# The opening of a hybrid attention / DeltaNet layer on one core: another order of modulation vectors, transposes and first projections

## The chip, the core and the metric

The kernel runs on one core of a Trainium2 chip. A core has TensorE (PE in the profile; its weight loads are PEld), VectorE (DVE), ScalarE (ACT), GpSimd (POOL), and SyncE (SP), which here only starts transfers. Each engine works through its own instructions in a fixed order and waits at an instruction until the inputs of that instruction are there. The metric is the device time of one execution in microseconds (us).

## The reference, cut to what matters

The program is one layer over 512 latent tokens `x` and 256 context tokens `ctx`, 1024 channels wide, in float32. The change is in the very first part of it: the modulation vectors, the modulated normalised inputs, and the beginning of the big input projection.

```python
mod_lat = jax.nn.silu(c) @ w_mod + b_mod              # 1024 -> 6 x 1024
mod_ctx = jax.nn.silu(c_ctx) @ w_mod + b_mod
sh1, sc1, g1, sh2, sc2, g2 = jnp.split(mod_lat, 6, axis=-1)
csh1, csc1, ... = jnp.split(mod_ctx, 6, axis=-1)

hx = rms_norm(x)   * (1.0 + sc1)  + sh1               # (512, 1024)
hc = rms_norm(ctx) * (1.0 + csc1) + csh1              # (256, 1024)
... = split_cols(hx @ w_in)                           # attention q/k/v, DeltaNet q/k/v, decays, gates
... = split_cols(hc @ w_in[:, :CTX_COLS])
```

Behind that stand grouped-query attention, a bidirectional chunked DeltaNet, the merge of both, an output projection, a gated MLP with a short convolution, and a final RMSNorm. Nothing of that part is changed.

## The kernel before, in words

Every product of the projections is made of three matmuls, because a float32 operand is taken as a high part and a low part: `hi` is a copy in the format that TensorE reads (ScalarE, line 127), `lo` is the difference (line 115, VectorE, or GpSimd where an engine is named). The helper `split` (line 129) does both, and `mm3` issues the three matmuls `w_hi x_hi`, `w_hi x_lo`, `w_lo x_hi`. A weight tile is 128 x 1024; its parts are called `whi` and `wlo`, what was loaded is `wraw`.

The opening (lines 440 to 605) goes through these steps, and each has a letter in the string `ORD`, which sets the order in which TensorE's work of the opening is issued. TensorE's instructions are pinned to that order; on the other engines a scheduler orders the instructions by priority when the program is built, and on the SP queue the loads are pinned to the order of `LORD`.

- Loads, by SP, in the order `x0 x1 x2 w0 w1 h0 h1 w2 .. w7`: the context and the two halves of `x` (tiles `xs`, 1 MB each), the first third of `w_mod` in eight tiles `wm` of 1 MB, and two weight tiles `h0`, `h1` of the projection. Then the rotary tables (`tabs`), `wrow`, and, in a place that the scheduler chooses, the masks (`cst`, line 474). Eight transfers can be on the way; the ninth waits for the first.
- Each `xs` tile holds two rows of tokens per partition. ScalarE squares and sums the one row, VectorE the other (lines 487, 488), VectorE and GpSimd make the reciprocal root `rs` (the power is on GpSimd, line 115), and VectorE scales both rows (line 493).
- `xN` (N from 0 to 11): TensorE transposes four 128 x 128 blocks of an `xs` tile into a PSUM tile `pt`; ScalarE or VectorE copies them to a stash (`hxL`, `hcL`). There are two `pt` buffers. `x0` to `x3` are the context, `x4` to `x7` the first and `x8` to `x11` the second half of the tokens.
- `aN`, `bN`: the two halves of the vector product number N (0 to 3) of `silu(c)`, `silu(c_ctx)` with 512 columns of `w_mod` (`pm`); after `bN` ScalarE copies the result into `mrow`. Product N needs the tiles `wm` 2N and 2N+1. There is one `pm` buffer.
- `mN`: makes columns (one value per partition) of the row `mrow`: four matmuls against a 0/1 matrix `sel` into `xb`, which also add up the four partial sums, and two additions of the bias (`mod`, `modc`).
- `yN`: the modulation of the channel pair N (channels 256N to 256N+255): `hf` for the latent tokens on VectorE, for the context on ScalarE, then the split of four tiles (`hxH`, `hcH` on ScalarE, `hxL`, `hcL` on VectorE).
- `pK` (K from 0 to 7): the matmuls of both projection tiles (heads) with channel block K: for each head three on the context (`pc`, 256 columns) and three on the latent tokens (`mb`, 512 columns). `qK` and `rK` are the halves of `pK` for head 0 and head 1; the string of before uses neither.
- `dN`: 4N matmuls on zeros, whose result nobody uses.

So the products of a channel block need the modulation of that block, that needs its columns, these the vector product, and that two tiles of `w_mod`. After the last product `p7`, convolution taps are read from the PSUM tiles by ScalarE and VectorE, and TensorE goes on with the attention's K, V and Q blocks (`pq`).

Of the kernel before, what the change touches and what calls it, by code (L numbers as in the profile page):

```python
# [16 lines left out]
KT = 8  # L17
# [17 lines left out]
POOLW = 0  # L35
ND, D0U = 4, 6
KV = 10
ORD = 'd4 x0 x1 x2 x3 x4 x5 x6 x7 a0 x8 x9 x10 x11 b0 d1 m0 y0 a1 p0 b1 p1 m1 y1 a2 b2 p2 m2 y2 p3 a3 b3 p4 m3 y3 p5 p6 p7'
RK = 1.0
HB = 2  # L40
WS = [1.0, 1.0, 1.0]
# [34 lines left out]
def hybrid_layer_body(tc, x, ctxt, xT, consts, cols, rows, w_mod1, w_mod2, w_av, w_aq, w_cm, w_pa, w_pd, w_out,  # L76
# [64 lines left out]
    with es:  # L141
# [299 lines left out]
        with m1_es:  # L441
# [11 lines left out]
            for op in LORD.split():  # L453
                i = int(op[1])
                with sooner():
                    if op[0] == "w":
                        wms.append(m1.tile([P, 4, 512], F32, name="wm", tag="in", bufs=WB))
                        ordered_load(wms[i], w_mod1[i // 2, i % 2])
                    elif op[0] == "h":
                        h, part = order[i]  # L460
                        raw = ws.tile([P, 1024], F32, name="wraw", tag="wraw", bufs=2)
                        ordered_load(raw, w_cm[8 * part + h])
                    else:
                        xs.append(m1.tile([P, 2, D], F32, name="xs", tag="in", bufs=WB))
                        ordered_load(xs[i], x[:, 2 * i - 2:2 * i, :] if i else ctxt)
                if op[0] == "h":
                    with first():
                        hi, lo = (m1.tile([P, 1024], F32R, name=n, tag=n, bufs=NS) for n in ("whi", "wlo"))
                        split(hi, lo, raw)
                        hw.append((hi, lo))  # L470
            with sooner():
                ordered_load(tabs.rearrange("p a b -> p (a b)"), consts[:, C_COS:C_END])
                ordered_load(wrow, rows[0:512].partition_broadcast(P))
            SP.dma_start(cst[:, C_MS:C_TRI], consts[:, C_MS:C_TRI])
            cs = m1.tile([P, 16], F32, name="cs")
            act(cs, col[:, S_C:S_C + 16], AF.Tanh, scale=0.5)
            stt(cs, cs, 1.0, col[:, S_C:S_C + 16], ALU.add, ALU.mult)
            cs32 = m1.tile([P, KT, 32], F32, name="cs32")
            G.memset(cs32, 0.0)
            ts(cs32[:, :, 0:2], cs.rearrange("p (k two) -> p k two", two=2), 0.5, ALU.mult)  # L480
            sel = m1.tile([P, 2], F32, name="sel")
            V.tensor_reduce(out=sel, in_=ident.rearrange("p (b c) -> p c b", c=32)[:, 0:2, :], axis=AX.X, op=ALU.add)
            ss = m1.tile([P, 6], F32, name="ss")
            rs = m1.tile([P, 6], F32, name="rs")
            for i in range(3):
# [4 lines left out]
                sl = slice(2 * i, 2 * i + 2)  # L490
                rsqrt(rs[:, sl], ss[:, sl], 1.0 / D, EPS)
                for t in range(2):
                    ts(xs[i][:, t, :], xs[i][:, t, :], rs[:, 2 * i + t:2 * i + t + 1], ALU.mult)
            m2 = lambda t, o: t[:, o:o + 16].rearrange("p (s k) -> p s k", s=2)
            wsl = lambda k: slice(k * P, k * P + P)

# [9 lines left out]
                    act(mrows[nb], ps)  # L506

            def mod_cols(nb, mrow):
                pst = xbank()[:, 0, 0:8].rearrange("p (a b) -> p a b", b=2)
                for i in range(4):  # L510
                    mm(pst[:, i, :], mrow[:, i * P:(i + 1) * P], sel)
                ks = slice(2 * nb, 2 * nb + 2)
                p4 = pst.rearrange("p (s k) r -> p s k r", s=2)
                for j, md in enumerate((mod, modc)):
                    tt(m2(md, 0)[:, :, ks], p4[:, :, :, j], m2(col, S_BMOD)[:, :, ks], ALU.add)

# [35 lines left out]
            def early_proj(k, heads=slice(0, NS)):  # L552
                if not hps:
                    for _ in range(NS):
                        hps.append((mbank(), mps.tile([P, NCX], F32, name="pc", tag="pc", bufs=NS)))
                for (ps, pc), (hi, lo) in list(zip(hps, hw))[heads]:
                    mm3(pc, hi[:, wsl(k)], lo[:, wsl(k)], hcH[:, k, :], hcL[:, k, :], k, KT)
                    mm3(ps, hi[:, wsl(k)], lo[:, wsl(k)], hxH[:, k, :], hxL[:, k, :], k, KT)

            pinned[0] = True  # L560
            mrows, mpm = {}, {}
# [1113 lines left out]
```

## Time and profile before

| | |
|---|---|
| median of 3 runs | 1242.44 us (1237.12 to 1246.0) |
| the profiled execution | 1239.93 us, of which the span from the first to the last instruction is 1238.2 us |
| granted TensorE clock, mean | 0.986 |
| busy time | PE 1183.2 us (96%), DVE 818.8 (66%), ACT 601.7 (49%), POOL 248.3 (20%) |
| the opening ends (last matmul of `p7` out, `pq` starts) | near 56 us of the span |

A row of the timeline gives start, duration, engine, line, operation, output and input tiles, shapes and a count, and in square brackets the idle time of the engine just before it with what ended it. A row of a stage gives for each engine its busy time and the number of instructions, then the granted TensorE clock (1.00 is full), the share of the time in which the DMA engines were busy, and the rate in GB/s. Matmuls overlap: the duration of one is longer than its distance from the next. Line numbers in rows are those of the kernel before.

### The profile page before, as it was taken

What the parts mean: (1) busy time and instruction counts of PE and PEld (TensorE: products, weight loads), DVE (VectorE), ACT (ScalarE), POOL (GpSimd) and SP (SyncE); (2) the same over time, 40 slices, a digit from 0 to 9 for tenths busy, and PEclk for the clock granted to TensorE, in tenths of its full rate; (3) what the DMA queues carried; (4) which work ended last, traced back from release to release, by engine and by line L of the source; (5) the groups of instructions that cost most, each with busy time, mean ns of one, the idle gap of its engine ahead of it and who ended that gap; (6) DMA issues with size and microseconds to landing.
All of it is one profiled execution on the core that took longest, in us unless ns stands there. A gap on an engine that the chain in (4) does not pass through costs nothing.

```text
span 1238.2 us, 20489 instructions
## 1 busy us (share of the span) xinstructions
PE 1183.2 (96%) x7753; PEld 1015.6 (82%) x7753; DVE 818.8 (66%) x1611; ACT 601.7 (49%) x1386; POOL 248.3 (20%) x334
## 2 busy tenths in 40 slices
PE   7999899999899898999999989999999999999996
PEld 5799888989787787788887678789888888888886
DVE  5648678888698657766657677866776765553333
ACT  4524477877565845744535432333544444432321
POOL 0111110100314695595574000000000000000000
PEclk8999999999999998999999999999999999999998
DMA  9413313332536426335336776862333422333331
GB/s 385 143 60 117 99 56 97 113 100 89 191 130 213 132 90 205 116 122 194 129 97 202 243 251 204 304 223 103 119 122 133 136 93 95 102 92 97 94 94 68
DMA packets 67554, 174.97 MB, mean 141 GB/s; under 512 B 7456, under 2 KB 18176, under 8 KB 66048
## 3 DMA queue, kind: packets, MB, share of 16 engines
q1 hardware_dynamic: 67456, 173.67, 41.8%
q8 instruction: 61, 1.00, 0.3%
q14 instruction: 37, 0.30, 0.1%
HBM read 146.85 MB, written 26.79 MB: 140 GB/s over the span
## 4 chain that ended last, share of the span: by engine, by line
PE 53%; DMA 4%; DVE 4%; ACT 2%; issue 1%; POOL 1%; SPq 0%; POOLq 0%; DVEq 0%; ACTq 0%
PE mc L84 33%; PE mb L84 13%; PE pb L84 5%; DMA gt<-atd 1%; DVE wlo L115 1%; DMA M<-gamdr 1%; PE pk L84 1%; ACT whi L127 0%; DMA wl<-in_w_mod_dram 0%; PE pqk L84 0%; DMA sz<-gdr 0%; POOL NN L115 0%; DMA cw<-in_rows_dram 0%; DMA Gb<-gamdr 0%; DMA NN<-gamdr 0%
## 5 line engine op out<-in xcount | busy, mean ns | idle before, releaser
L115 DVE TENSOR_TENSOR wlo<-wraw,whi 128x1024 fp32r<-128x1024 f32 (+1 forms) x153 | 188.7, 1235 | 159.9 <-ACT whi L127 159.5
L127 ACT ACTIVATE whi<-wraw 128x1024 fp32r<-128x1024 f32 (+1 forms) x153 | 159.5, 1044 | 213.8 <-PE mc L84 114.0
L84 PE MATMUL mc<-h,whi 128*128 128x512 f32 (+1 forms) x752 | 219.6, 376 | 0.3 <-ACT whi L127 0.3
L84 PE MATMUL mb<-hxH,whi 128*128 128x512 f32 x384 | 162.5, 423 | 1.6 <-DVE t L124 1.6
L84 PEld LDWEIGHTS mc<-h,whi 128*128 128x128 f32 x752 | 138.0, 188 | 26.1 <-ACT whi L127 0.5
L84 PE MATMUL mb<-hxL,whi 128*128 128x512 f32 x384 | 152.2, 396 | 0.2 <-DVE hxL L115 0.2
L84 PE MATMUL mb<-hxH,wlo 128*128 128x512 f32 x384 | 152.2, 396 | 0.0
L84 PE MATMUL mc<-h,wlo 128*128 128x512 f32 (+1 forms) x376 | 141.3, 376 | 0.5 <-DVE wlo L115 0.5
L84 PE MATMUL mc<-a,whi 128*128 128x512 f32 (+1 forms) x396 | 111.1, 366 | 0.6 <-DVE x L124 0.6
L115 POOL TENSOR_TENSOR rc<-rc,mhalf 128x2 f32<-128x2 f32 x4 | 3.0, 740 | 456.8 <-DVE rc L121 456.8
L84 PEld LDWEIGHTS mb<-hxH,wlo 128*128 128x128 f32 x384 | 73.0, 190 | 16.8
L84 PEld LDWEIGHTS mb<-hxH,whi 128*128 128x128 f32 x384 | 73.4, 191 | 11.9 <-issue 2.0
L84 PEld LDWEIGHTS mc<-a,whi 128*128 128x128 f32 x396 | 71.5, 189 | 12.9 <-DVE x L124 0.8
L84 PEld LDWEIGHTS mc<-h,wlo 128*128 128x128 f32 x376 | 70.8, 188 | 13.6 <-DVE wlo L115 1.0
L84 PEld LDWEIGHTS mb<-hxL,whi 128*128 128x128 f32 x384 | 73.5, 191 | 9.7 <-DVE hxL L115 0.5
L84 PE MATMUL mc<-a,wlo 128*128 128x512 f32 (+1 forms) x198 | 72.3, 365 | 0.0
L124 DVE SCALAR_TENSOR_TENSOR u<-mc,col,u 128x511 f32<-128x511 f32 x88 | 65.3, 746 | 1.4
L115 POOL TENSOR_TENSOR prod<-X,R 128x31 f32<-128x31 f32 (+15 forms) x93 | 55.5, 597 | 19.1 <-DVE X L115 12.3
L115 POOL TENSOR_TENSOR R<-R,prod 128x31 f32<-128x31 f32 (+15 forms) x93 | 56.5, 607 | 6.8
L84 PE MATMUL pq<-whi,hxH 128*128 128x256 f32 (+1 forms) x192 | 55.5, 289 | 0.0
L84 PE MATMUL pq<-wlo,hxH 128*128 128x256 f32 (+1 forms) x192 | 54.3, 283 | 0.1
L84 PE MATMUL pq<-whi,hxL 128*128 128x256 f32 (+1 forms) x192 | 54.2, 282 | 0.0
(323 smaller groups left out, 2692.1 us busy)
## 6 DMA issues: line engine op xcount, KB each, us to landing
wraw<-in_w_cm_dram SPq DMA_DIRECT2D x48, 512.0 KB, 3.6
wraw<-in_w_up_dram SPq DMA_DIRECT2D x44, 512.0 KB, 3.3
wl<-in_w_mod_dram SPq DMA_DIRECT2D x24, 512.0 KB, 4.9
wm<-in_w_mod_dram SPq DMA_DIRECT2D x8, 1024.0 KB, 16.6
wraw<-in_w_down_dram SPq DMA_DIRECT2D x16, 512.0 KB, 3.5
wraw<-in_w_aq_dram SPq DMA_DIRECT2D x10, 512.0 KB, 3.8
M<-gamdr SPq DMA_DIRECT2D x64, 64.0 KB, 4.5
wraw<-in_w_pa_dram SPq DMA_DIRECT2D x8, 512.0 KB, 4.4
```

The source lines that it names most:

```text
L84: i = nc.tensor.matmul(*a, **k)
L115: put((eng or V).tensor_tensor(out=out, in0=a, in1=b, op=op))
L124: V.scalar_tensor_tensor(out=out, in0=a, scalar=s, in1=b, op0=op0, op1=op1)
L127: put(A.activation(out, a, f, **kw))
```

## The change

Five edits, all in the opening.

- `ORD` is another string. There are 28 matmuls on zeros ahead of `x0` instead of 16, and the four of `d1` stand behind `x3` instead of behind `b0`. `b0` stands behind `x8`, ahead of `x9`; `m0` and `y0` stand behind `x9`, ahead of `x10` and `x11`. From then on both halves of a vector product stand ahead of the products they used to follow: `p0 a1 b1`, and the column form `m1` comes between the two heads of the product `p1` (`q1 m1 y1 r1`); so with `m2` and `m3`.
- The column form: instead of four matmuls with `sel`, four transposes of 128 x 128 blocks of `mrow` into one PSUM tile, then one VectorE sum over the four partial rows into `m4`, and the two bias additions read `m4`. `sel` and the reduction that made it are gone.
- The scaling of the second row of each `xs` tile is on GpSimd; the first stays on VectorE.
- The low part of the weight tile `h0` is made on GpSimd; that of `h1` stays on VectorE.
- The masks are loaded behind `wrow`, pinned in the SP order. Within `pK`, `qK` and `rK` the latent products come first, those on the context second.

```diff
-ORD = 'd4 x0 x1 x2 x3 x4 x5 x6 x7 a0 x8 x9 x10 x11 b0 d1 m0 y0 a1 p0 b1 p1 m1 y1 a2 b2 p2 m2 y2 p3 a3 b3 p4 m3 y3 p5 p6 p7'
+ORD = 'd7 x0 x1 x2 x3 d1 x4 x5 x6 x7 a0 x8 b0 x9 m0 y0 x10 x11 p0 a1 b1 q1 m1 y1 r1 a2 p2 b2 q3 m2 y2 r3 a3 p4 b3 q5 m3 y3 r5 p6 p7'
@@ loads of the weight tiles h0, h1
-                        split(hi, lo, raw)
+                        act(hi, raw)
+                        tt(lo, raw, hi, ALU.subtract, V if hw else G)
                         hw.append((hi, lo))
@@ masks
-            SP.dma_start(cst[:, C_MS:C_TRI], consts[:, C_MS:C_TRI])
+                ordered_load(cst[:, C_MS:C_TRI], consts[:, C_MS:C_TRI])
@@ sel
-            sel = m1.tile([P, 2], F32, name="sel")
-            V.tensor_reduce(out=sel, in_=ident.rearrange("p (b c) -> p c b", c=32)[:, 0:2, :], axis=AX.X, op=ALU.add)
@@ scaling of xs
-                    ts(xs[i][:, t, :], xs[i][:, t, :], rs[:, 2 * i + t:2 * i + t + 1], ALU.mult)
+                    ts(xs[i][:, t, :], xs[i][:, t, :], rs[:, 2 * i + t:2 * i + t + 1], ALU.mult, eng=G if t else V)
@@ mod_cols
-                pst = xbank()[:, 0, 0:8].rearrange("p (a b) -> p a b", b=2)
+                pst = xbank()
                 for i in range(4):
-                    mm(pst[:, i, :], mrow[:, i * P:(i + 1) * P], sel)
+                    transpose(pst[:, i, :], mrow[:, i * P:(i + 1) * P])
+                m4 = m1.tile([P, 4, 2], F32, name="m4", tag="m4", bufs=2)
+                V.tensor_reduce(out=m4, in_=pst.rearrange("p i (b c) -> p i c b", c=32)[:, :, 0:2, :], axis=AX.X, op=ALU.add)
                 ks = slice(2 * nb, 2 * nb + 2)
-                p4 = pst.rearrange("p (s k) r -> p s k r", s=2)
+                p4 = m4.rearrange("p (s k) r -> p s k r", s=2)
@@ early_proj
-                for (ps, pc), (hi, lo) in list(zip(hps, hw))[heads]:
+                some = list(zip(hps, hw))[heads]
+                for (ps, pc), (hi, lo) in some:
+                    mm3(ps, hi[:, wsl(k)], lo[:, wsl(k)], hxH[:, k, :], hxL[:, k, :], k, KT)
+                for (ps, pc), (hi, lo) in some:
                     mm3(pc, hi[:, wsl(k)], lo[:, wsl(k)], hcH[:, k, :], hcL[:, k, :], k, KT)
-                    mm3(ps, hi[:, wsl(k)], lo[:, wsl(k)], hxH[:, k, :], hxL[:, k, :], k, KT)
```

Three places of the built order, before and after. First VectorE at the beginning, around the first column form; `hxL<-pt` are copies of transposes, `wlo` is the low part of a weight tile, `mod` and `modc` are the columns. Before:

```order
L119 TENSOR_SCALAR xs<-xs,rs 128x1024 x2
L531 COPY hxL<-pt 128x2x256 x2
L115 TENSOR_TENSOR wlo<-wraw,whi 128x1024 x2
L115 TENSOR_TENSOR mod<-xb,col 128x2x2
L115 TENSOR_TENSOR modc<-xb,col 128x2x2
L121 TENSOR_SCALAR hf<-hxL,mod 128x512 x2
```

Now:

```order
L119 TENSOR_SCALAR xs<-xs,rs 128x1024
L532 COPY hxL<-pt 128x2x256 x2
L115 TENSOR_TENSOR wlo<-wraw,whi 128x1024
L512 TENSOR_REDUCE m_402<-xb 128x8
L115 TENSOR_TENSOR mod<-m_402,col 128x2x2
L115 TENSOR_TENSOR modc<-m_402,col 128x2x2
L532 COPY hxL<-pt 128x2x256
L121 TENSOR_SCALAR hf<-hxL,mod 128x512 x2
```

One of the two weight differences and one scaling have gone from this stretch (to GpSimd), the new sum `m4` (shown as `m_402`) stands behind the other weight difference, and one copy of transposes now stands between the columns and the modulation `hf`.

Second TensorE behind the second column form `m1`. Before, both halves of the next vector product and then the products of the next pair follow it:

```order
L84 MATMUL xb<-sel,mrow 128x2 x4
L84 MATMUL pm<-wm,cs_259 32x512 x8
L84 MATMUL pc<-hcH,whi 128x256
L84 MATMUL pc<-hcL,whi 128x256
L84 MATMUL pc<-hcH,wlo 128x256
```

Now one head's products of the pair before, half a vector product, and then the next pair:

```order
L88 MATMUL xb<-cst,mrow 128x128 x4
L84 MATMUL mb<-hxH,whi 128x512
L84 MATMUL mb<-hxL,whi 128x512
L84 MATMUL mb<-hxH,wlo 128x512
L84 MATMUL pc<-hcH,whi 128x256
L84 MATMUL pc<-hcL,whi 128x256
L84 MATMUL pc<-hcH,wlo 128x256
L84 MATMUL pm<-wm,cs_259 32x512 x4
L84 MATMUL mb<-hxH,whi 128x512
```

What stands between the column form and the first product that needs it is another set of instructions.

Third ScalarE in the third and fourth modulation; `whi<-wraw 128x1024` here are the high parts of two weight tiles (`w_aq`) of the K block that comes after the opening. Before, they stand behind the last vector row `mrow`:

```order
L127 ACTIVATE mrow<-pm 128x512
L127 ACTIVATE hf<-hcL,modc 128x256 x2
L127 ACTIVATE hxH<-hf 128x512
L127 ACTIVATE hcH<-hf 128x256
L127 ACTIVATE hxH<-hf 128x512
L127 ACTIVATE hcH<-hf 128x256
L127 ACTIVATE mrow<-pm 128x512
L127 ACTIVATE whi<-wraw 128x1024 x2
```

Now they stand one modulation earlier, the first ahead of it and the second inside it:

```order
L127 ACTIVATE mrow<-pm 128x512
L127 ACTIVATE whi<-wraw 128x1024
L127 ACTIVATE hf<-hcL,modc 128x256 x2
L127 ACTIVATE hxH<-hf 128x512 x2
L127 ACTIVATE whi<-wraw 128x1024
L127 ACTIVATE hcH<-hf 128x256 x2
L127 ACTIVATE whi<-wraw 128x864
L127 ACTIVATE mrow<-pm 128x512
```

VectorE's differences `wlo` of the same tiles have moved with them. Behind `p7` TensorE's order is the same instruction by instruction in both programs; on VectorE and ScalarE a few neighbours are exchanged there.

## The prediction

> **What bounds the kernel now.** I read the page first, then the stages, TensorE's waits, and the timeline. The page's first line:
>
> ```profile
> span 1238.2 us, 20489 instructions
> ```
>
> The profiled execution took 1239.93 us, 1.7 us more than this span. The opening is its first 56 us. The stages (columns: length, busy time of PE, PEld, DVE, ACT, POOL, granted clock, DMA share, GB/s) and, in shorter ones, the clock:
>
> ```profile
> 0.00:9.80 9.80, 5.33 (x16) 3.96 (x17) 3.54 (x12) 3.24 (x5) 1.36 (x10) 1.00 0.80 305
> 9.80:27.04 17.24, 14.85 (x85) 9.21 (x85) 12.45 (x22) 10.41 (x20) 1.40 (x2) 0.80 1.02 422
> 27.04:56.05 29.01, 27.21 (x160) 19.17 (x161) 15.10 (x33) 14.56 (x29) 0.81 (x1) 0.94 0.55 202
> 56.05:140.00 83.95, 83.90 (x699) 83.65 (x698) 57.70 (x206) 35.07 (x132) 13.34 (x13) 1.00 0.26 82
> ...
> 14.70:18.10 3.40, 3.40 (x18) 2.37 (x20) 2.25 (x6) 0.99 (x3) 0.70 (x1) 0.50 1.01 414
> ...
> 28.30:31.80 3.50, 3.50 (x13) 2.18 (x16) 0.38 (x2) 0.00 (x0) 0.00 (x0) 0.51 1.01 417
> ```
>
> To 27.04 us, where the first product starts, transfers run at full rate and TensorE waits for normalised inputs and columns. Behind 56.05 it is busy 83.90 of 83.95 us: nothing there hides or adds to a shift, so a microsecond of the opening is a microsecond of the kernel. From 27.04 to 56.05:
>
> ```profile
> PE pc L84 <- ACT hcH L127: 1.8, 2, 1.3
> PE pc L84 <- DVE hcL L115: 1.1, 3, 0.4
> PE mb L84 <- DVE hxL L115: 0.2, 1, 0.2
> ...
> 33.63 0.28 PE L84 MATMUL pc<-hcH,whi 128*128 128x256 f32 x1
> 34.68 0.95 PE L84 MATMUL xb<-sel,mrow 128*128 128x2 f32 x8
> 35.56 1.92 PE L84 MATMUL pm<-wm,cs 128*32 128x512 f32 x16
> ...
> 1.49 5.33 PE L84 MATMUL pt<-hxH 128*128 128x512 f32 x16 [1.49 <-DVE hxH L563]
> 17.87 1.16 PE L84 MATMUL pm<-wm,cs 128*32 128x512 f32 x8
> 18.96 1.13 PE L88 MATMUL pt<-cst,xs 128*128 128x128 f32 x8
> 21.45 1.06 PE L84 MATMUL pm<-wm,cs 128*32 128x512 f32 x8
> ```
>
> 1.3 us of the first wait lie ahead of 27.04, so 1.8 us of waits are inside. One head of one block takes 34.68 - 33.63 = 1.05 us, a half vector product (1.92 - 0.15 tail)/2 = 0.88, a column form 0.95, four transposes 0.46 and a tail of 0.2. The 29.0 us are 16 x 1.05 = 16.8, plus 6 x 0.88 = 5.3, plus 3 x 0.95 = 2.85, plus 1.7 lost to the clock of 0.51 in 3.5 us, and 2.35 of idle time and gaps. TensorE's own work sets this stage, with its waits well covered.
>
> **Up to the first product.** Prices on ScalarE, VectorE and GpSimd, and the loads that are waited for:
>
> ```profile
> 11.05 1.09 ACT L127 ACTIVATE hcL<-pt 128x512 f32<-128x512 f32 x2 [0.69 <-PE pt L88]
> 13.34 1.05 ACT L127 ACTIVATE hxH<-xs 128x1024 fp32r<-128x1024 f32 x1
> 23.00 0.59 ACT L127 ACTIVATE mrow<-pm 128x512 f32<-128x512 f32 x1
> 25.06 1.09 ACT L127 ACTIVATE hf<-hcL,modc 128x256 f32<-128x256 f32 x2 [1.47 <-DVE modc L115]
> 26.06 0.62 ACT L127 ACTIVATE hxH<-hf 128x512 fp32r<-128x512 f32 x1
> 46.37 2.00 ACT L127 ACTIVATE whi<-wraw 128x1024 fp32r<-128x1024 f32 x2
> ...
> 3.75 0.17 DVE L482 TENSOR_REDUCE sel<-cst 128x2 f32<-128x8 f32 x1 [2.31 <-DMA cst<-in_consts_dram]
> 8.99 1.42 DVE L119 TENSOR_SCALAR xs<-xs,rs 128x1024 f32<-128x1024 f32 x2 [0.82 <-POOL rs L115]
> 21.73 1.22 DVE L115 TENSOR_TENSOR wlo<-wraw,whi 128x1024 fp32r<-128x1024 f32 x1
> 24.74 0.16 DVE L115 TENSOR_TENSOR mod<-xb,col 128x4 f32<-128x4 f32 x1 [0.37 <-PE xb L84]
> 24.94 1.00 DVE L121 TENSOR_SCALAR hf<-hxL,mod 128x512 f32<-128x512 f32 x2
> 26.71 0.69 DVE L115 TENSOR_TENSOR hxL<-hf,hxH 128x512 fp32r<-128x512 f32 x1 [0.77 <-ACT hxH L127]
> ...
> xs<-in_x_dram SPq DMA_DIRECT2D x1, 1024.0 KB, 9.0
> 2.13 0.91 SPq L448 DMA_DIRECT2D xs<-in_x_dram  x2
> ```
>
> The twelve further matmuls on zeros cost nothing: 16 take 5.33 us from 1.49 (12 more at that rate end at 10.8, at the later spacing near 9.4), and x0 is held anyway: on ScalarE the square of the third `xs` tile now stands ahead of the copies of transposes. That tile lands at 2.6 + 9.0 = 11.6, the square ends at 12.7, and the first `pt` buffer is free (copies of 0.5 each) only from 13.3. x2 and x3 follow, then d1; x4 starts at 15.5, and four groups at half clock (to 18.1 as in the row of before; about 0.85 each, a little under twice 0.46) bring a0 to 18.9 instead of 17.87. x8 and b0 follow without x9 to x11: b0 starts at 20.3 instead of 21.45. ScalarE first makes both `whi` (1.0 each, 19.6 to 21.5), then `mrow`, at 21.5 against 23.00; its transposes end at 22.8, where the columns of before were read at 24.74. That gains 1.9 us.
>
> GpSimd's new work is not in this trace in its form. Its nearest rows, and one place where both engines use SBUF:
>
> ```profile
> L990 POOL MEMSET R<- 128x1024 f32 x4 | 3.8, 955 | 0.0
> L1033 POOL COPY TTm<-o_tr 32x384 f32<-32x384 f32 x16 | 9.1, 569 | 1.2 <-PE pb L84 0.5
> L115 POOL TENSOR_TENSOR kA<-tabs,wrow 128x512 f32<-128x512 f32 x1 | 1.3, 1291 | 38.6 <-PE mb L84 38.6
> ...
> 511.37 2.13 DVE L115 TENSOR_TENSOR wlo<-wraw,whi 128x1024 fp32r<-128x1024 f32 x1
> 512.37 2.85 POOL L115 TENSOR_TENSOR NN<-NN,cst 128x768 f32<-128x768 f32 x1
> 516.25 1.85 POOL L115 TENSOR_TENSOR NN<-NN,Gb 128x768 f32<-128x768 f32 x1
> ```
>
> A scaling of 128x1024 lies between a memset of the size (0.96) and a two-input operation, 1.29 per 512 columns or 2.6; I take 1.4, the copy's 0.57 for 384 columns carried on, since it too reads one tensor. The difference `wlo` has two inputs: 1.85/768 x 1024 = 2.45. The last three rows show exclusion: the VectorE difference that takes 1.22 alone took 2.13 beside GpSimd's sums, and GpSimd's next 2.85 instead of 1.85 behind it.
>
> If the scalings exclude each other too, a pair takes up to 0.75 + 1.4; but the copy of x0 waits for 12.7 and x4 for 15.5, which covers it. Exclusion decides at the weight differences: GpSimd's runs from 20.7 to 23.1; VectorE's, whose `whi` is there at 21.6, goes from 23.1 to 24.3, and the sum stands behind it, as VectorE's order shows. The sum has no row; it lies between the 0.17 of the old reduction and the 0.69 of a 512-column operation, and with 8 results out of 32 numbers I take 0.22. Columns at 24.7; then ScalarE's two `hf` (0.55 each), a copy (0.5) and an `hcH` (0.35) stand ahead of `hxH` (0.62): first product at 27.3, 0.3 later than before. Without exclusion the sum is at 22.8 and the first product at 25.9: 1.1 earlier. I take the exclusion.
>
> **From the first product on.** The columns cost 0.46 instead of 0.95, three times: -1.45. The clock first, since it can undo that:
>
> ```profile
> 24.90:28.30 3.40, 1.69 (x12) 0.70 (x5) 2.63 (x8) 2.75 (x6) 0.00 (x0) 1.00 1.02 414
> ```
>
> Before, 1.69 us of work in 3.4 ahead of 28.3 were followed by 3.5 us at half clock. Now TensorE has done x11 by 23.6 and stands still until 27.3, so about 1.1 us of work fall into the same stretch: I take one slow stretch, worth 1.75 us, as before: +0.05.
>
> The idle time grows. From the start of a column form to the first product that needs it pass: transposes 0.65, sum and columns 0.45, two context `hf` on ScalarE 1.05 and `hxH` 0.62, with signals 2.9 us. Before, the work of TensorE that stood there was 0.95 + 1.76 = 2.7 us for m1, 0.95 + 2.1 + 1.76 = 4.8 for m2, 0.95 + 2.1 = 3.05 for m3. Now it is 0.46 + 1.05 + 0.88 = 2.4 for m1 and m2, and 1.5 for m3, behind which no vector product is left. So TensorE stands 0.5, 0.5 and 1.4 us, and each time 0.55 more after one matmul, until the low part `hxL` (0.69) is made. In y2 the K weights come in between, as ScalarE's order shows:
>
> ```profile
> 24.18 2.81 SPq L214 DMA_DIRECT2D wraw<-in_w_aq_dram  x2
> ...
> wraw<-in_w_aq_dram SPq DMA_DIRECT2D x1, 512.0 KB, 15.9
> ```
>
> The first lands at 24.18 + 15.9 = 40.1 (the bytes ahead of it are the same, since the masks only move behind `wrow`), ScalarE copies it at 41.6, behind the third `mrow`, so nobody waits for the load; but the two VectorE differences of 1.22 stand ahead of `hxL` and of the context's low part, so p4 waits 0.3 more for the one and 0.85 for the other. Idle: 0.55 (p0), 1.05 (p2), 2.2 (p4), 1.9 (p6), together 5.6 before rounding. I walked both orders through engine by engine, with these durations and 0.05 us for a signal; for the order of before this ends the opening at 56.0, where the trace has 56.05. For the new order: 27.3 + 16.8 + 5.3 + 1.4 + 1.75 + 5.6 = 58.15. The sum: start +0.3, columns -1.45, clock +0.05, idle and gaps 5.6 - 2.35 = +3.25: **+2.1 us**, 0.2% of the kernel.
>
> At nothing: the masks, which nothing in the opening reads; the order latent before context in `p`, the same matmuls; the SP queue, whose loads stand behind a backlog of 15 us anyway (w5 to w7 come 0.6 us earlier, and b3 runs near 48, 12 us behind them).
>
> [...]
>
> **The rivals.** *Faster:* no exclusion between the engines. First product at 25.9, 1.1 earlier, and with 2.1 us of work ahead of 28.3 the clock may stay full. But then ScalarE reaches the copy of the K weights before 40.1 and waits: the end is 56.0, and 54.9 if the tile lands a microsecond sooner, 54.0 with a full clock from 14.7 on: 0 to -2 us. For it: one-input work on GpSimd isn't seen beside VectorE here; against: two-input work is, and the weight difference is that. *Slower, by GpSimd's chain:* each power for `rs` now stands behind the scaling of the tile before on GpSimd, so three scalings in a row lead to x8 and to the first columns. From about 3 us for a scaling this chain is the later one, and each further microsecond costs three; 1% (12.4 us) is reached near 6. The longest row that compares, 1.29 for half the size with two inputs, makes 2.6, and the end 59.0: +2.9. [...] *Not what it says:* if y0 needed x9 to x11, an earlier b0 would gain nothing; but y0 reads what x0, x4 and x8 left, so the edit holds: chance 0.
>
> **The numbers.** Forecast, +2.1 (from +1 to +3): 0.5; faster, 0 to -2: 0.33; slow clock 0.12; GpSimd's chain beyond +3: 0.05. Against the profiled 1239.93 that is 1242.0, against the median, 2.5 above it, 1244.5; I give 1243, between the two. The three runs spread from 1237.12 to 1246.0, so the range is 1237.12 - 1 to 1246.0 + 3: 1236 to 1249. A measurement tells about 1%, 12.4 us, from no change. Even with the first product at 25.9 and no idle time behind it the opening would end at 25.9 + 23.5 = 49.4, 6.7 us earlier, so faster by 1% can only come from outside the opening: 0.02. Slower by 1% needs GpSimd at 6 us: 0.03. Same: 0.95.
>
> **What would show it.** In the profile after: the third square ahead of the first copy on ScalarE; a GpSimd scaling of 1.0 to 2.6 us; VectorE's first weight difference near 2.4 us, or starting when GpSimd's ends; first product at 27 to 28 us; a granted clock of 0.50 for one window behind it; TensorE idle for 5 to 6 us between there and `pq`, most of it at p4 and p6; `pq` at 57 to 59 us. A first product at 26 us with `pq` at 56 or earlier would show the faster rival, one behind 29 the chain on GpSimd. The prediction is wrong if `pq` starts below 54 or above 61, or if the time differs by more than the opening's end does.

## The result, and the profile after

The changed kernel takes 1248.05 us (median of 11 runs, 1245.34 to 1249.7), the kernel before 1239.71 us (11 runs): a ratio of 1.0065, 95% interval 1.0051 to 1.0078, or 6.3 to 9.7 us more. The forecast was 1243, in a range that holds the result; the +2.1 us of its working are a quarter of the 8.1 measured.

The profiled execution of after took 1246.63 us. First the page's first line, then the stages (length, busy time of PE, PEld, DVE, ACT, POOL, granted clock, DMA share, GB/s), cut at the first product and at the first `pq` as before:

```profile
span 1244.9 us, 20486 instructions
...
9.80:29.83 20.03, 13.11 (x76) 8.90 (x74) 12.11 (x20) 10.98 (x20) 13.78 (x6) 0.83 1.02 422
29.83:61.26 31.43, 28.23 (x157) 18.54 (x158) 15.39 (x34) 14.47 (x28) 0.18 (x1) 0.95 0.43 152
61.26:145.21 83.95, 82.74 (x690) 82.36 (x689) 58.52 (x206) 34.49 (x127) 14.00 (x13) 1.00 0.25 82
```

The first product starts at 29.83 instead of 27.04 (+2.8; forecast 27.3), `pq` at 61.26 instead of 56.28 (the first `pq` matmul; +5.0; the forecast's 58.15 was worked against 56.05). GpSimd, 1.40 us busy in the second stage before, is now busy 13.78 of 20.03 us. Behind the opening TensorE, which was busy 83.90 of 83.95 us, is idle for 1.2 us. The waits of TensorE (us in total, times, longest) in and just behind the products:

```profile
PE mb L84 <- ACT hxH L127: 4.9, 4, 3.2
...
PE pq L84 <- DVE rk L121: 1.2, 1, 1.2
...
PE mb L84 <- DVE hxL L115: 1.0, 3, 0.5
```

3.2 of the first lie ahead of 29.83. The second is new, and stands in no step of the prediction. The start, in the order of time (start, length, engine, line; POOL is GpSimd; from here on the line numbers of a row are those of the kernel that it comes from):

```profile
8.31 0.70 POOL L115 TENSOR_TENSOR rs<-rs,mhalf 128x2 f32<-128x2 f32 x1 [7.13 <-DVE rs L121]
9.04 0.75 DVE L119 TENSOR_SCALAR xs<-xs,rs 128x1024 f32<-128x1024 f32 x1 [0.81 <-POOL rs L115]
9.11 4.46 POOL L119 TENSOR_SCALAR xs<-xs,rs 128x1024 f32<-128x1024 f32 x1
...
11.05 0.80 DVE L121 TENSOR_SCALAR rs<-ss 128x2 f32<-128x2 f32 x1
...
13.54 0.72 POOL L115 TENSOR_TENSOR rs<-rs,mhalf 128x2 f32<-128x2 f32 x1
13.62 3.56 PE L88 MATMUL pt<-cst,xs 128*128 128x128 f32 x15 [3.23 <-POOL xs L119]
...
14.37 3.41 POOL L119 TENSOR_SCALAR xs<-xs,rs 128x1024 f32<-128x1024 f32 x1
...
17.74 0.72 POOL L115 TENSOR_TENSOR rs<-rs,mhalf 128x2 f32<-128x2 f32 x1
18.56 2.85 POOL L119 TENSOR_SCALAR xs<-xs,rs 128x1024 f32<-128x1024 f32 x1
...
23.45 2.37 POOL L115 TENSOR_TENSOR wlo<-wraw,whi 128x1024 fp32r<-128x1024 f32 x1 [2.04 <-ACT whi L127]
...
24.35 2.55 DVE L115 TENSOR_TENSOR wlo<-wraw,whi 128x1024 fp32r<-128x1024 f32 x1 [0.25 <-ACT whi L127]
24.44 0.60 ACT L127 ACTIVATE mrow<-pm 128x512 f32<-128x512 f32 x1
...
26.83 0.18 DVE L512 TENSOR_REDUCE m<-xb 128x8 f32<-128x32 f32 x1
```

GpSimd's scalings take 4.46, 3.41 and 2.85 us, and the powers `rs` stand between them at 8.31, 13.54 and 17.74: one chain on one engine. The transposes of the context wait 3.23 us for its first link. At the end VectorE's weight difference takes 2.55 us beside GpSimd's, and the sum stands behind it, as the prediction had it.

One profiled execution below, that of the first experiment, was disturbed (its clock was 0.84 on average), so only its times are used; the other thirteen traces are used whole.

### The profile page after: what moved, and what is told of

Same layout as the page of the kernel before. It is cut to its first block, busy times and chain, and to the rows that moved or that the text cites. A ratio compares the mean times of both kernels' runs of the same rounds, so it can differ in the third digit from the quotient of the medians.

```text
span 1244.9 us, 20486 instructions
## 1 busy us (share of the span) xinstructions
PE 1188.7 (95%) x7749; PEld 1020.5 (82%) x7749; DVE 819.1 (66%) x1610; ACT 601.2 (48%) x1386; POOL 262.5 (21%) x338
## 4 chain that ended last, share of the span: by engine, by line
PE 53%; DVE 4%; DMA 3%; issue 1%; POOL 1%; ACT 1%; SPq 0%; POOLq 0%; DVEq 0%; ACTq 0%
PE mc L84 33%; PE mb L84 13%; PE pb L84 6%; DMA wl<-in_w_mod_dram 1%; DVE wlo L115 1%; PE pk L84 1%; PE pqk L84 0%; DMA szd<-co 0%; DMA gt<-atd 0%; DMA M<-gamdr 0%; POOL NN L115 0%; DVE o_tr L1016 0%; DMA sz<-gdr 0%; ACT whi L127 0%; DMA cw<-in_rows_dram 0%
## 5 line engine op out<-in xcount | busy, mean ns | idle before, releaser
L115 DVE TENSOR_TENSOR wlo<-wraw,whi 128x1024 fp32r<-128x1024 f32 (+1 forms) x152 | 188.8, 1243 | 157.0 <-ACT whi L127 154.5
L84 PE MATMUL mb<-hxH,whi 128*128 128x512 f32 x384 | 165.3, 430 | 6.5 <-ACT hxH L127 4.9
L115 POOL TENSOR_TENSOR prod<-X,R 128x31 f32<-128x31 f32 (+15 forms) x93 | 53.3, 573 | 19.8 <-DVE X L115 12.9
L124 DVE SCALAR_TENSOR_TENSOR t<-mb,col,t 128x511 f32<-128x511 f32 (+1 forms) x76 | 48.9, 644 | 9.7 <-ACT t L127 9.4
```

Of the source, the lines that this page charges most:

```text
L84: i = nc.tensor.matmul(*a, **k)
L115: put((eng or V).tensor_tensor(out=out, in0=a, in1=b, op=op))
L124: V.scalar_tensor_tensor(out=out, in0=a, scalar=s, in1=b, op0=op0, op1=op1)
```

## The experiments

Each is after, or before, with one thing changed, or two or three where its name says so. The table has, for each, the ratio to before with its 95% interval (before ran again beside the experiments, after did not), and from its trace the start of the first product and of `pq`, and what the time between them leaves when its work is taken off: 16 x 1.05 for the products, 0.88 for each half vector product (5.3 for six in the new order of steps, 4.4 for five in the old one), three column forms (2.85, or 1.4 with transposes), and half of the time that the clock stood at 0.5 in between (an estimate: in before the next latent matmul of a row starts 0.42 us behind the last one there, 0.23 to 0.24 at full clock). The sixth half, `a1`, stands ahead of the first product in the old order, here in before, where that product starts at 27.04:

```profile
24.63 1.06 PE L84 MATMUL pm<-wm,cs 128*32 128x512 f32 x8
```

The prediction's sum for before takes off six. The rest is idle time and gaps. It is more than the idle time of the profile, which grows from 1.8 us (29.01 - 27.21) to 3.2 (31.43 - 28.23): a latent matmul ahead of a wait counts as busy for 0.49 us, though in a row the next one starts 0.23 behind it.

| kernel | ratio (interval) | first product | `pq` | clock at 0.5 between, us | rest, us |
|---|---|---|---|---|---|
| before | 1 | 27.04 | 56.28 | 3.4 | 3.5 |
| after | 1.0065 (1.0051 to 1.0078) | 29.83 | 61.26 | 3.4 | 6.2 |
| after, scalings on VectorE | 1.0028 (1.0012 to 1.0044) | - | - | - | - |
| after, weight differences on VectorE | 1.0042 (1.0025 to 1.0058) | 28.35 | 59.88 | 3.4 | 6.3 |
| after, both on VectorE | 1.0038 (1.0024 to 1.0053) | 27.91 | 59.93 | 3.4 | 6.8 |
| after, both on VectorE, context first | 1.0051 (1.0032 to 1.0070) | 25.08 | 61.40 | 6.8 | 9.4 |
| after, context first | 1.0050 (1.0030 to 1.0071) | 28.98 | 64.67 | 10.2 | 7.1 |
| after, half a scaling on GpSimd | 1.0052 (1.0031 to 1.0073) | 28.51 | 62.16 | 6.8 | 6.7 |
| after, old order of steps | 1.0063 (1.0045 to 1.0080) | 31.68 | 60.74 | 3.4 | 4.8 |
| before, scalings on GpSimd | 1.0043 (1.0025 to 1.0060) | 31.59 | 61.30 | 3.4 | 4.0 |
| before, new order of steps | 1.0050 (1.0031 to 1.0070) | 27.90 | 62.68 | 6.8 | 6.4 |
| before, new column form | 0.9995 (0.9978 to 1.0013) | 26.86 | 55.71 | 3.4 | 4.6 |
| before, latent first | 1.0007 (0.9986 to 1.0027) | 27.18 | 54.03 | 0 | 2.8 |
| early columns, old cover | 0.9976 (0.9956 to 0.9997) | 26.26 | 52.94 | 0 | 4.1 |

An interval is some 2 us to either side, and a trace is one execution: the column on the clock may be another in the next one, as the mean clock is (0.981 to 0.988 over the 11 runs of after).

### GpSimd's scalings and weight difference

After, with the scalings on VectorE:

```diff
-ts(xs[i][:, t, :], xs[i][:, t, :], rs[:, 2 * i + t:2 * i + t + 1], ALU.mult, eng=G if t else V)
+ts(xs[i][:, t, :], xs[i][:, t, :], rs[:, 2 * i + t:2 * i + t + 1], ALU.mult)
```

> The kernel after, with all six scalings back on VectorE; the GpSimd weight difference, the order of steps, the column form and the order of the products stay as after. Theory A (the price of GpSimd's scaling, 2.7 to 4.5 us instead of the 1.4 taken, makes the chain of powers and scalings late): the first product starts near 27.3 us instead of 29.83, and pq near 58.5 instead of 61.26, so that some 2.5 to 3 us of the 8.1 come back (about 1245). Theory B (the scalings are covered and the new order of steps alone makes the opening longer): the first product may come earlier, but pq still starts at 60.5 or later, and less than 1 us comes back.

The time is 4.6 us below after (1.0065 - 1.0028, of 1239), more than theory A's 2.5 to 3, with an interval of 2 us or more to either side, and against B's "less than 1". Of the starts that both theories name nothing can be said here. The same one line put into before, alone:

> The kernel before, with only the second scaling of each tile moved to GpSimd. Theory A (the scaling costs 2.7 to 4.5 us on GpSimd and VectorE's work beside it is held up, in any order of steps): scalings of 4.4, 3.4 and 2.8 us, the first product starts 3 to 4.5 us later than 27.04, pq at 59 to 60.5, and the time is 3 to 5 us above before. Rival (the scalings hurt only in the new order, where each power stands behind a scaling and the copies wait): first product at most 1.5 us later, less than 1.5 us in the time.

It costs 5.3 us (3.1 to 7.4), `pq` at 61.30, the start 4.55 later: theory A, a little above its upper ends. Its start, where the order of steps is the old one:

```profile
9.09 4.45 POOL L119 TENSOR_SCALAR xs<-xs,rs 128x1024 f32<-128x1024 f32 x1
...
14.34 3.40 POOL L119 TENSOR_SCALAR xs<-xs,rs 128x1024 f32<-128x1024 f32 x1
...
18.53 3.40 POOL L119 TENSOR_SCALAR xs<-xs,rs 128x1024 f32<-128x1024 f32 x1
```

VectorE's own scaling runs beside each from some 0.07 us earlier on and takes 0.75, as it did alone; 3.40 less the 0.68 that overlap is 2.7. This is an estimate: no run has this operation of GpSimd without one of VectorE's scalings beside it. To see whether the price or the neighbourhood matters, GpSimd gets half of each row block:

```diff
+for c, e in ((slice(0, D), V),) if t == 0 else ((slice(0, D // 2), V), (slice(D // 2, D), G)):
+    ts(xs[i][:, t, c], xs[i][:, t, c], rs[:, 2 * i + t:2 * i + t + 1], ALU.mult, eng=e)
```

> The kernel after, with GpSimd scaling only the second half (512 columns) of the second row block of each tile, and VectorE the first half as well: a GpSimd scaling then takes about half of its 2.7 to 2.9 us, which is the 1.4 us that the prediction had taken for the whole. Theory A (the price of the scaling is the one term that was mis-sized at the start): the first product starts at 27 to 28 us (forecast 27.3) instead of 29.83, and the time is 2.5 to 4 us below after. Rival (it is not the price but any GpSimd work on SBUF beside VectorE that stretches the chain): first product at 29 or later, less than 1 us below after.

```profile
9.08 2.12 POOL L119 TENSOR_SCALAR xs<-xs,rs 128x512 f32<-128x512 f32 x1
...
16.77 2.12 POOL L119 TENSOR_SCALAR xs<-xs,rs 128x512 f32<-128x512 f32 x1
...
18.94 1.97 PE L88 MATMUL pt<-cst,xs 128*128 128x128 f32 x8 [2.93 <-DVE hxL L533]
```

All three take 2.12, or 1.4 without the 0.7 beside VectorE's first scaling: half the size, half of 2.7. By this estimate a scaling of 1024 columns costs some 2.7 us of GpSimd, and one that starts some 0.07 us behind VectorE's takes 0.7 more, as if it did not get on until that is done. But the two don't always exclude each other. In the next run, with both weight differences on VectorE, VectorE's third scaling lies in the middle of GpSimd's and takes its usual time, and GpSimd's takes 2.86:

```profile
18.52 2.86 POOL L119 TENSOR_SCALAR xs<-xs,rs 128x1024 f32<-128x1024 f32 x1
...
19.64 0.74 DVE L119 TENSOR_SCALAR xs<-xs,rs 128x1024 f32<-128x1024 f32 x1
```

In after GpSimd's third takes as long, 2.85, while VectorE's, begun 2.0 us behind it, takes 1.40. What decides between these cases isn't shown. The first product of the run with half a scaling is at 28.51, between the two theories: the next transposes wait 2.93 us for a copy behind VectorE's scalings, and the stretch in which they wait is followed by one at half clock, from 18.5 to 21.9 (8 transposes in 1.97 us above). In the time 1.6 us come back, with an interval that holds none and 4: this run supports the price, and leaves open what it is worth.

After, with both weight differences on VectorE:

```diff
-tt(lo, raw, hi, ALU.subtract, V if hw else G)
+tt(lo, raw, hi, ALU.subtract)
```

> The kernel after, with both weight differences on VectorE. Theory A (VectorE's difference waits out GpSimd's, as the trace shows with 2.55 us instead of 1.22): two differences of 1.22 in a row end about 0.8 us earlier than 26.90, so the first product starts near 29.0 instead of 29.83 and pq near 60.4. Rival: the columns' transposes (25.1 to 25.7) and ScalarE's queue end last, and the first product moves by less than 0.3.

```profile
22.48 1.23 DVE L115 TENSOR_TENSOR wlo<-wraw,whi 128x1024 fp32r<-128x1024 f32 x1 [1.32 <-ACT whi L127]
23.51 0.60 ACT L127 ACTIVATE mrow<-pm 128x512 f32<-128x512 f32 x1
...
24.22 1.22 DVE L115 TENSOR_TENSOR wlo<-wraw,whi 128x1024 fp32r<-128x1024 f32 x1
25.35 0.18 DVE L512 TENSOR_REDUCE m<-xb 128x8 f32<-128x32 f32 x1
```

Each takes 1.22, the sum is at 25.35 instead of 26.83, the first product 1.5 earlier and `pq` 1.4, and the time is 2.9 us below after (1.0065 - 1.0042): theory A, which had 0.8 for the start. Of the 1.5, 0.9 lie ahead of the differences (`mrow` at 23.51 instead of 24.44, in a trace with one window at half clock less ahead of it); from `mrow` to the sum it is 1.84 us instead of 2.39, so the exclusion itself is worth some 0.6 here. With scalings and differences on VectorE:

> The kernel after, with the scalings and both weight differences on VectorE: what is left of the change is the order of steps, the column form, the order latent before context, and the masks. Theory A (GpSimd's share is what the start of the products lost, 3.0 us by the scalings and 1.5 by the difference as the two runs with one of them undone show): the first product starts at 25.0 to 26.0, pq at 56.5 to 57.5, the wait for rk of about 1.1 us behind it stays, and the time is 0 to 2 us above before. Rival (the new order of steps gives back what an earlier start gains, since its columns wait for loads and copies): pq not before 58.5, 3 us or more above before.

The rival: `pq` at 59.93, and 3.0 to 6.6 us above before, though nothing of the change is left on GpSimd. The start, 27.91, has a stretch at half clock from 19.3 to 22.7 ahead of it; the kernel with the context products first, below, has none there and starts at 25.08 with a product on the context, and at 26.90 with its first latent one. And the rest behind the first product is 6.8 us: the order of steps by itself costs, as the run with the order alone shows below, and theory A had left that out.

### The order of steps

```diff
-ORD = 'd7 x0 x1 x2 x3 d1 x4 x5 x6 x7 a0 x8 b0 x9 m0 y0 x10 x11 p0 a1 b1 q1 m1 y1 r1 a2 p2 b2 q3 m2 y2 r3 a3 p4 b3 q5 m3 y3 r5 p6 p7'
+ORD = 'd4 x0 x1 x2 x3 x4 x5 x6 x7 a0 x8 x9 x10 x11 b0 d1 m0 y0 a1 p0 b1 p1 m1 y1 a2 b2 p2 m2 y2 p3 a3 b3 p4 m3 y3 p5 p6 p7'
```

This diff makes after with the old order; the reverse of it, in before, is the new order alone.

> The kernel after, with the old order of steps (4 + 1 groups of zero matmuls, x9 to x11 ahead of b0, two blocks of products held back as cover for the columns); scalings, difference, column form and masks as after. Theory A (the new order leaves TensorE 5.6 us idle behind the first product, the old one 2.35): the first product starts later, at 30 to 31.5, but from there to pq it takes 27.6 (29.0 less 3 x 0.46) instead of 31.4, so that pq starts at 57.6 to 59.5 and 2 to 3.5 us come back. Rival (the new order's earlier b0 and columns are worth as much as the idle time): pq within 0.7 of 61.26.

The rival: `pq` is 0.5 earlier, the time the same. The rest falls from 6.2 to 4.8, less than A says, and `a1` stands ahead of the first product again, but the start moves from 29.83 to 31.68, since in the old order `b0` waits for x9 to x11, whose tile GpSimd's chain makes last.

> The kernel before, with only the new order of steps. Theory A (the order itself costs: an earlier start of the products by 1 to 2 us, then 3 us or more of further idle time of TensorE at the columns of blocks 2 and 3, and perhaps one more stretch at half clock behind an idle time of 2 us or more): first product at 25 to 26.5, pq at 57.5 to 60, the time 3 to 6 us above before. Rival (the order costs only together with GpSimd's late scalings): pq at 55.5 to 57, the time within 1.5 us of before.

6.2 us (3.8 to 8.7), theory A in the time and a little above it, by another way: no earlier start, but a rest of 6.4 instead of 3.5, two stretches at half clock, and `pq` at 62.68 instead of 57.5 to 60. One of them, with its cause (a wait of TensorE, then three windows):

```profile
56.23 0.39 PE L84 MATMUL pc<-hcH,whi 128*128 128x256 f32 x1 [1.97 <-ACT hcH L127]
```

```profile
50.10:53.50 3.40, 3.40 (x26) 2.43 (x26) 1.46 (x4) 0.66 (x2) 0.00 (x0) 1.00 0.69 188
53.50:56.90 3.40, 1.15 (x5) 0.46 (x3) 2.90 (x6) 3.40 (x7) 0.00 (x0) 1.00 0.33 88
56.90:60.30 3.40, 3.32 (x10) 2.89 (x11) 0.96 (x3) 0.10 (x1) 0.00 (x0) 0.50 0.18 71
```

It is the wait at p6 behind `m3`, with no vector product left as cover. TensorE does 1.15 us in 3.4, and the next 3.4 are at 0.50. So the order alone costs about as much as the scalings alone, and the two together are less than their sum: with the scalings late, the new order starts earlier than the old one (29.83 against 31.6), which pays part of its idle time.

### The order of the products

After, with the old order in a block, for each head context and then latent:

```diff
-some = list(zip(hps, hw))[heads]
-for (ps, pc), (hi, lo) in some:
-    mm3(ps, ..., hxH[:, k, :], hxL[:, k, :], k, KT)
-for (ps, pc), (hi, lo) in some:
+for (ps, pc), (hi, lo) in list(zip(hps, hw))[heads]:
     mm3(pc, ..., hcH[:, k, :], hcL[:, k, :], k, KT)
+    mm3(ps, ..., hxH[:, k, :], hxL[:, k, :], k, KT)
```

> The kernel after, with the products of a block in the old order (for each head the context's, then the latent ones). Theory A (with the latent products first, VectorE's order has the SiLU product co of the first head ahead of the last context tap of the second head, so that rk and the transposed K tiles come late): pq starts at 61.3 as after, give or take 0.4, the wait of TensorE for rk of 1.2 us in the pq stage is gone, and the time is some 1.2 us lower. Rival (the order of the products is free, as the prediction said, and the 1.2 us come from elsewhere): the wait for rk is still there at 1.0 to 1.4 us and the time is the same.

The wait for `rk` is gone. But `pq` starts at 64.67, which neither expected: the rest is 7.1 instead of 6.2 and 10.2 us of the products stand at half clock. The time is 1.9 us lower, with an interval that also holds no difference. In before, the latent products first, alone:

> The kernel before, with only the order latent before context in each block of products. Theory A (its cost lies behind the opening, in VectorE's order, where a SiLU product gets ahead of the last context tap): pq at 56.3 give or take 0.5, a wait of TensorE for rk of 1.0 to 1.3 us in the pq stage that before does not have, the time 1 to 1.5 us above before. Rival (free, as the prediction said): no such wait, the same time.

```profile
PE pq L84 <- DVE rk L121: 1.1, 1, 1.1
```

The wait appears, 1.1 us, at the same place (`pq` itself is at 54.03, in a trace without a stretch at half clock among the products); the time is 1.0007, which allows the wait and allows none. Its chain in after, ScalarE's order and VectorE's:

```profile
67.46 0.85 ACT L127 ACTIVATE co<-t 128x768 f32<-128x768 f32 x1 [2.06 <-DVE t L124]
```

```profile
65.43 1.54 DVE L124 SCALAR_TENSOR_TENSOR co<-co,t 128x768 f32<-128x768 f32 x1 [0.58 <-ACT co L127]
66.89 0.47 DVE L124 SCALAR_TENSOR_TENSOR t<-pc,col,t 128x255 f32<-128x255 f32 x1
68.34 0.96 DVE L124 SCALAR_TENSOR_TENSOR co<-co,t 128x768 f32<-128x768 f32 x1 [0.97 <-ACT co L127]
69.21 0.16 DVE L121 TENSOR_SCALAR rk<-kss 128x2 f32<-128x2 f32 x1
```

and in before:

```profile
62.07 0.16 DVE L121 TENSOR_SCALAR rk<-kss 128x2 f32<-128x2 f32 x1
```

With the context products last, the scheduler put the SiLU product `co` of the first head ahead of the second head's last context tap `t<-pc`. That tap, 0.47 us, therefore runs at 66.89, ScalarE waits 2.06 for it, and the norm `rk` comes 7.95 us behind the first `pq` (69.21 - 61.26) instead of 5.8 (62.07 - 56.28). The wait stands in all six traces with the latent products first, at 1.1 or 1.2 us, and in none with the context first.

After with context first, and GpSimd's work on VectorE:

> The kernel after, with scalings and differences on VectorE and the products of a block in the old order, context before latent: what is left is the order of steps, the column form and the masks. Theory A (with the old order of products TensorE waits for the context's high part behind each column form, as the run with that part alone undone shows with 4.85 us of idle time instead of 3.20, but the wait for rk goes): first product at 25 to 26, pq at 58 to 59.5, no wait for rk, and the time within 1 us of the kernel with the latent products first. Rival (the order of the products is worth nothing in the opening): pq as with the latent products first, and 1.2 us faster by the wait for rk.

No wait for `rk`, as both say, but `pq` at 61.40 instead of 58 to 59.5. It has the earliest start of all, 25.08, and the largest rest, 9.4: what starts earlier waits longer at p2, p4 and p6. The time, 1.0051, is within 1.6 us of the kernel with the latent products first.

### The column form, and a version from the parts that help

In before, only the four transposes and the sum:

> The kernel before, with only the column form by transposes and a sum. Theory A (each column form takes 0.46 us of TensorE instead of 0.95, the sum adds 0.2 on VectorE to the way to the columns, and the cover of the old order holds): from the first product to pq 27.8 to 28.4 us instead of 29.2, first product between 26.7 and 27.1, pq near 55, the time 1 to 1.5 us below before. Rival (the added sum makes the columns later by as much as TensorE saves, so that TensorE waits instead): pq within 0.4 of 56.3, the same time.

The rival in the time, 0.9995. 1.45 us of TensorE's work are gone, 1.1 come back as idle time and gaps (4.6 instead of 3.5), and `pq` is 0.6 earlier, between the two.

The last kernel has before with this column form and

```diff
-ORD = 'd4 x0 x1 x2 x3 x4 x5 x6 x7 a0 x8 x9 x10 x11 b0 d1 m0 y0 a1 p0 b1 p1 m1 y1 ...
+ORD = 'd4 x0 x1 x2 x3 x4 x5 x6 x7 a0 x8 b0 x9 m0 y0 x10 x11 a1 d2 p0 b1 p1 m1 y1 ...
```

and the old string from `b1` on.

> A version put together from the parts that help: the kernel before with the column form by transposes and the sum, the second half of the first vector product (b0) and the first columns ahead of x10 and x11, two groups of zero matmuls ahead of the first product instead of the one ahead of the columns, and from there on the old order with its two blocks of products as cover; nothing on GpSimd, context before latent, masks as before. Theory A (an earlier start is kept where the cover stays): first product at 25.0 to 25.8 instead of 27.04, no stretch at half clock right behind it, pq at 53 to 54.5, the time 2 to 3.5 us below before. Rival (an earlier start runs into later loads and columns): pq not before 55.5, the time within 1 us of before.

`pq` starts at 52.94, 3.3 us earlier than in before, and the time is 0.9976 (0.9956 to 0.9997), 0.4 to 5.5 us below before: theory A in sign and size, though its upper end is close to none. Of the 3.3 us, 1.7 are the window at half clock that the trace of before has behind its start and this one has not, and the profiled execution, 1241.64, is the longest of the 12 of this kernel: the trace shows an earlier `pq`, not the gain of the whole. The start is at 26.26 and not 25.0 to 25.8, because the zero matmuls run until then; for that the window ahead of it is full, and the clock stays:

```profile
22.60:26.00 3.40, 3.40 (x23) 2.11 (x21) 3.37 (x9) 3.40 (x8) 0.00 (x0) 1.00 1.00 411
26.00:29.40 3.40, 3.40 (x22) 2.02 (x20) 1.58 (x4) 0.41 (x1) 0.00 (x0) 1.00 1.05 413
```

## Why the forecast had the sign and not the size

**The start, +0.3 forecast, +2.8 measured: the step that failed.** It is the price of the scaling on GpSimd. I took 1.4 us between 0.96 and 2.6, by carrying on a copy of 32 partitions; it is some 2.7, a little above the upper end, which was a two-input operation of twice the row's size. And the exclusion between the scalings was called covered ("a pair takes up to 0.75 + 1.4; but the copy of x0 waits for 12.7 and x4 for 15.5, which covers it"): the three took 4.46, 3.41 and 2.85, TensorE waited for the first until 13.62, and `mrow`, forecast at 21.5, came at 24.44. At that price the chain of powers and scalings is the later one. That was the rival with a chance of 0.05: it was to begin "From about 3 us for a scaling", and the three took 3.6 on average; its sign, a first product behind 29, is there.

**The exclusion at the weight differences: right.** 2.55 and 2.37 us, one behind the other in effect, the sum behind them; undone, each takes 1.22.

**The columns and the idle time: right together, from a misread base.** The sum has -1.45 + 3.25 from a base of 2.35. That base took off six half vector products where five stand behind the first product of before, so its idle time and gaps were 3.2, and 0.9 of the 3.25 is the half that the new order moves behind the first product. The total of the walk doesn't change by this. Measured: -1.45 + 0.9 + (6.2 - 3.5) = +2.15 instead of +1.8. In the profile's own count TensorE is idle for 3.2 us there, not for 5 to 6, and 2.7 of them are at p4 and p6, as said. That the order costs this much even without GpSimd the run with the order alone shows (rest 6.4). The sum took 0.18, for 0.22 forecast.

**The clock: right in after, wrong as a term.** One slow stretch of 3.4 us, worth 1.7, stands behind the start in after as forecast. But of the seven traces with the new order four have two or three, of the six with the old order none has more than one: where TensorE waits longer (rests of 6.2 to 9.4 us in the new order, 2.8 to 4.8 in the old one), slow stretches were more frequent. That is 1.7 windows on average against 0.7, so by these few traces the term should have been up to +1.8, not +0.05. No run shows the slow clock that had a chance of 0.12: in after the clock is back at 1.00 from 19.8, as in before from 18.1, behind a window that was filled to the end (3.42 us busy), though with zero matmuls in it; the window under the hardware has transposes alone.

**At nothing: one of the three failed.** "The order latent before context in `p`, the same matmuls" is the same for TensorE's work, but it turned VectorE's order behind the opening, 1.1 to 1.2 us of TensorE's time. That nothing behind `pq` hides a shift holds, that nothing adds to it does not: the first and the last `pq` matmul of one kind (their first and last start), before:

```profile
L84 PE MATMUL pq<-whi,hxH x192: 276/281/369, 61.9 to 141.8; 128*128 128x256 f32 x160, 128*128 128x288 f32 x32
```

and after:

```profile
L84 PE MATMUL pq<-whi,hxH x192: 276/281/369, 66.9 to 148.0; 128*128 128x256 f32 x160, 128*128 128x288 f32 x32
```

5.0 us become 6.2. The masks and the twelve zero matmuls were not tried alone.

**The sum.** Of 8.1 us, 5.0 are the opening (start 2.8, the rest 2.2), 1.2 the wait for `rk`. 1.9 us (0.1 to 3.5 by the interval) stay open. The pair of traces can't show most of them: its spans differ by 6.7 us (1244.9 and 1238.2), so only 0.5 lie behind that wait, and the profiled execution of after, 1246.63, is 1.4 below the median of after. Behind the opening the clock stands at 0.5 for eight windows of 3.4 us instead of five, and yet the two spans are only 0.5 further apart at the end. Whether the change makes such windows more frequent isn't shown, since the traces of all kernels have four to nine without a pattern.

**The base.** 1243 stood on three runs with a median of 1242.44; over 11 runs before is 1239.71. The forecast was nearer to the result by that than by its working. That the range holds the result is luck: its upper end came from the highest of those three runs, 1246.0. The working's own +1 to +3 on 1239.71 gives 1240.7 to 1242.7. By its own signs the prediction is wrong, since `pq` at 61.26 is above 61, and the time differs by 8.1 us where the opening's end moved by 5.0. And a measurement tells less than the 1% it took: the interval here is 0.14% to either side.

## What to carry to other kernels

Price an operation on another engine by a row with the same kind of operation over all partitions, and if there is none take the dearest neighbour, not the nearest in name; where a row shows that the two engines exclude each other, add the other's time to it. When a stage is taken apart into a sum, count the instructions in its own window: here one half vector product of the base lay outside it. Idle time of TensorE was paid twice where it filled most of a clock window (of the 60 at full clock that were busy for less than 0.45, 58 were followed by one at 0.5), so an order that starts earlier but uses up its cover can lose; zero matmuls in a wait that can't be avoided looked cheap in the last kernel, but were not tried alone. Look at the in-order engines behind a moved block too: the same matmuls in another order gave VectorE another queue.

## What the runs showed of the hardware

**When the clock falls.** In all thirteen traces the stretches at 0.5, but for one at the program's end, are one or two windows of 3.41 us, in a phase that differs from trace to trace (the first fall is at 11.29 us in before and at 12.94 in after). The first 350 windows of each trace, in its own phase, by TensorE's busy share in each (a shift of the phase by 0.06 us moves a count by up to four):

| granted clock in the window | busy share | windows | next one at 0.5 |
|---|---|---|---|
| 1.0 | below 0.45 | 60 | 58 |
| 1.0 | 0.45 to 0.6 | 88 | 37 |
| 1.0 | 0.6 and more | 4279 | 4 |
| 0.5 | below 0.8 | 19 | 19 |
| 0.5 | 0.8 to 0.9 | 11 | 5 |
| 0.5 | 0.9 and more | 93 | 0 |

So here some 1.9 us of idle time in a window of 3.41 were enough for the fall (58 of 60), and the clock came back behind all 93 windows at 0.5 that were busy for 0.9 and more, behind 6 of 11 between 0.8 and 0.9, and behind none of the 19 below. If the phase differs between executions of one kernel as it does between these traces, waits of about 2 us in sum cost up to 1.7 us more (half of 3.41) in some executions and not in others. That is an estimate, since no kernel has two traces here; the kernels spread by 4 to 12 us between their runs, of which this may be a part.

**A window of transposes.** Before with the scalings on GpSimd has a window with transposes alone (TensorE's rows, then its windows):

```profile
13.60 3.73 PE L88 MATMUL pt<-cst,xs 128*128 128x128 f32 x16 [3.30 <-POOL xs L119]
```

```profile
13.30:16.70 3.40, 3.10 (x14) 2.73 (x15) 0.83 (x2) 1.56 (x3) 3.30 (x3) 0.50 0.99 414
16.70:20.10 3.40, 1.83 (x13) 1.17 (x12) 1.35 (x2) 2.11 (x4) 3.30 (x3) 1.00 1.04 424
20.10:23.50 3.40, 3.40 (x17) 1.41 (x15) 2.05 (x3) 1.80 (x3) 1.83 (x1) 0.50 1.01 419
```

3.10 us of transposes at half clock, and the next window is at 1.00; 1.83 us of them in that one, and the next is at 0.50 again. In the table the one is a window at 0.5 that was busy for 0.91, behind which the clock came back 93 times of 93, the other one at 1.0 that was busy for 0.54, behind which it fell 37 times of 88.

**GpSimd beside VectorE.** By the estimate above a scaling costs GpSimd some 2.7 us for 1024 columns of fp32, no less than the operations with two inputs took (1.29 for 512, 2.37 for 1024), and 0.7 more where it starts some 0.07 us behind VectorE's. VectorE's sum of squares ran beside it in 1.22 us, as it does in before. An `rs` of two columns took 0.80 instead of 0.17 beside the first scaling, but 0.16 beside the second. Why the first scaling takes 1.05 longer than the second stays open; beside the first VectorE has two sums of squares and the long `rs`, beside the second the short `rs` alone.
